# A hybrid diffusion layer on one core: the first stage starts on a quarter of its modulation, and two tiles walk the weight rows together

## The chip, the cores and the metric

The kernel runs on one core of a Trainium2 chip. The metric is device time in microseconds (us) of one execution. The engines are named as in the profile: PE is TensorE (matmuls; PEld is its weight load), DVE is VectorE, ACT is ScalarE, POOL is GpSimd, SP is SyncE, which here only issues DMAs. `L427` is line 427 of the kernel.

## What is computed

One layer of a diffusion backbone, for 256 context ("prompt") tokens and 2048 latent ("sample") tokens, all float32, model width 1024. Cut to the part that the change touches:

- Each stream has its modulation: `mod = silu(c) @ w_mod + b_mod`, with `c` the conditioning vector of the latent stream and `c_ctx` that of the prompt stream. It has six chunks of 1024 columns: shift1, scale1, gate1, shift2, scale2, gate2. The first stage needs only shift1 and scale1, which are columns 0 to 2047 of `w_mod` (1024 rows): 8.4 MB.
- `h = RMSNorm(x) * (1 + scale1) + shift1`, then one projection `h @ w_in`, whose 2048 columns are four groups of 512: queries, keys, values and the Fourier channels. `w_in` is another 8.4 MB.
- Queries and keys get an RMS norm per head; latent ones also get a rotary embedding. The Fourier channels go through a two-dimensional DFT, queries, keys and values through differential attention with four heads (512 cached and 2048 own keys for the latent stream: 2560, or five blocks of 512). In differential attention two softmaxes P0 and P1 are combined as P0 + factor x P1 before they meet the values.
- Then an output projection and a squared-ReLU MLP, both far behind the change.

## The kernel before

**Tiles and precision.** The tokens are 18 tiles of 128 rows: tiles 0 and 1 are the prompt, 2 to 17 the latent stream. A product in full precision is three matmuls (`mm3`, L85 to L88): each operand is split in a high part (a cast to a shorter format) and a low part (the rest), and high x high, high x low and low x high are added up in one PSUM bank. So a projection of one tile and one group, `proj(i, g)` (L237), is 8 row blocks k x 3 = 24 matmuls of 512 columns. Matmuls of plain float32 operands take two records each in the trace.

**Who sets the order.** Within a block `with tc.manual_schedule()` each engine gets its instructions as the code states them. Outside it a planner orders them by its own estimates. The first stage consists of a block by hand (L409 to L519), a loop that the planner orders (L521 to L550), and another block by hand for the last tile and the passage to the second stage (from L553).

**The block by hand (L409 to L519).**

- `setup_small` (L90) loads the conditioning vectors, biases and norm gains as rows and turns them into columns, `cols`, by one transpose.
- SP loads x0, then `w_mod` by rows: `wm0` to `wm7` (L416), each 128 rows x 2048 columns, 1 MB, with x1 between. They lie in pools of their own; W's tiles take their memory when they are done.
- The modulation of all 2048 columns: groups 0 to 2 of 512 columns each are PE matmuls with `cols` as the two-column stationary operand, and give a row for each stream (L427: 24 float32 matmuls); group 3 is summed on DVE, multiplying each `w_mod` row block by a column of `cols` (L431, L433: eight operations per stream) with a sum over partitions by PE with `ones` (L461). `mod_cols` (L452 to L456) copies the three rows out of PSUM and transposes them back into columns. L464 adds the bias to all, `mk_scale` (L170) makes `scale1`.
- `load_gains` (L109) loads the small vectors for the query and key norms by POOL's queue. `setup_gains` (L117) turns them into the tiles `qg`, `kg` and the factor `nlam`; in the middle of it ACT takes an exponential (L127) that DVE waits for. It stands behind `proj(1, 1)`.
- Tile 0 is transposed by PE and modulated on ACT and DVE (`h_mod`, L469), split into `HH[0]`. Tile 1's transposes follow (L487), its modulation is spread over the walk.
- `w_in` arrives in halves of a row block (`w_half`, L443: 128 x 1024, 512 KB) in a ring of six buffers. For each row block k, ACT casts four high parts (L495), DVE forms four low parts (L496), and PE multiplies tile 0 with all four groups (12 matmuls). The split weights, 64 tiles of 128 x 512, stay in SBUF through the first stage: group 2 in a pool on the left (`p1w`, L210), the other groups in a pool on the right (`p1wr`, L436), where they lie by group, then high or low, then k.
- Behind the walk, `f_post(0)`, `v_out(0)`, `proj(1, 0)`, the norms of tile 0's queries and keys, `proj(1, 1)`, and x3's load (L510 to L519).

**The loop** (L521) runs i from 1 to 16. For each tile: norm of the next tile, its projections in four groups, `transposed(i + 1)` (L228: eight transposes, modulation, split), the post-processing of each group, and the transposes of the queries and keys of tile i − 1 (`qk_T`). PSUM banks with the tag `pt` (two) carry all transposes. On odd tiles it also computes another 512 columns of the modulation, `mod_load` and `mod_group_v` (L155): DVE's weighted sums, then their sum over partitions on PE, all within the same tile.

**The passage to the second stage.** `right.close()` (L564) gives back the memory of the right weight tiles; `fa` takes it for the Fourier operands: `d_load` (L593) loads differences and reversed rows by SP, `dft` (L577) the DFT matrices by POOL's queue. A load can go when the last matmul that reads the memory it overwrites is done. `e2048` (L618) forms the DFT's operands from them.

**Attention's first group.** A group is 256 queries of a head. PE computes scores (L918), DVE takes maxima by block (L923), ACT the exponentials (L942), and `combine` forms P0 + factor x P1. As a rule POOL does that (L964 multiplies, L965 adds, in pieces of 1024 and 1536 columns). For the second half of the very first group `vcomb = 5` (L891): DVE combines all five blocks of 512 (L954).

Of the kernel before, what the change touches and what calls it, by code (L numbers as in the profile page):

```python
# [18 lines left out]
P = 128  # L19
# [21 lines left out]
def body(tc, a, out):  # L41
    nc = tc.nc
    ctx = ExitStack()
    with ctx:
# [98 lines left out]
        def mod_group(t2, pps, gi, w):  # L143

            pr = pps.tile([P, 512], F32, tag="pg", name=f"pr{gi}")
            for k in range(KD):
                nc.tensor.matmul(pr[0:2, :], cols[:, k:k + 9:8], w[k // 2][:, k % 2, :], start=(k == 0), stop=(k == KD - 1))
            r = t2(f"mr{gi}")
            nc.scalar.copy(r[0:2, :], pr[0:2, :])
            pm = pps.tile([P, 4, 2], F32, tag="pm", name=f"pm{gi}")  # L150
            for j in range(4):
                nc.tensor.transpose(pm[:, j, :], r[0:2, j * P:(j + 1) * P], ident[0:2, 0:2])
            mod_bias(gi, pm)

        def mod_group_v(t2, pps, gi, w):  # L155

            pm = pps.tile([P, 4, 2], F32, tag="pm", name=f"pm{gi}")
            for s in range(2):
                acc = t2(f"macc{gi}_{s}")
                for k in range(KD):  # L160
                    wk, sc = w[k // 2][:, k % 2, :], cols[:, 8 * s + k:8 * s + k + 1]
                    if k == 0:
                        nc.vector.tensor_scalar_mul(acc, wk, sc)
                    else:
                        nc.vector.scalar_tensor_tensor(acc, wk, sc, acc, op0=ALU.mult, op1=ALU.add)
                for j in range(4):
                    nc.tensor.matmul(pm[:, j, s:s + 1], acc[:, j * P:(j + 1) * P], ones, start=True, stop=True)
            mod_bias(gi, pm)
# [39 lines left out]
        with ExitStack() as c1:  # L208
            p1 = c1.enter_context(tc.tile_pool(name="p1", bufs=2))
            wp = c1.enter_context(tc.tile_pool(name="p1w", bufs=1))  # L210
# [197 lines left out]
            wsrc = a["w_in"][0].rearrange("(k p) n -> p k n", p=P)  # L408
            with tc.manual_schedule():  # L409
                with tc.tile_pool(name="p0r", bufs=3) as rows, tc.tile_pool(name="p0m", bufs=KD - 3, side="right") as more:  # L410
                    setup_small(p1, pps)
                    load(0)
                    wm = []
                    for k in range(KD):
                        wm.append((rows if k < 3 else more).tile([P, 2048], F32, tag="row", name=f"wm{k}"))
                        nc.sync.dma_start(wm[k], wmod[:, k, 0:2048])  # L416
                        if k == 2:
                            load(1)
                    norm(p1, X[0], "a0")
                    pr = [pp.tile([P, 512], F32, tag="pj", name=f"pr{gi}", bufs=4) for gi in range(4)]  # L420
                    pt0 = [pp.tile([P, 4, P], F32, tag="pt", name=f"pta0_{b}") for b in range(2)]
                    for k in range(KD):
                        nc.tensor.transpose(pt0[k // 4][:, k % 4, :], X[0][:, k * P:(k + 1) * P], ident)
                    acc = [t2(f"macc3_{s}") for s in range(2)]
                    for k in range(KD):
                        for gi in range(3):
                            nc.tensor.matmul(pr[gi][0:2, :], cols[:, k:k + 9:8], wm[k][:, gi * 512:gi * 512 + 512], start=(k == 0), stop=(k == KD - 1))  # L427
                        for s in range(2):
                            wk, sc = wm[k][:, 1536:2048], cols[:, 8 * s + k:8 * s + k + 1]
                            if k == 0:  # L430
                                nc.vector.tensor_scalar_mul(acc[s], wk, sc)  # L431
                            else:
                                nc.vector.scalar_tensor_tensor(acc[s], wk, sc, acc[s], op0=ALU.mult, op1=ALU.add)  # L433
                        if k == 4:
                            norm(p1, X[1], "a1")
                wr = right.enter_context(tc.tile_pool(name="p1wr", bufs=1, side="right", reuse_waits="tile"))  # L436
                W = {(g, x): [(wp if g == 2 else wr).tile([P, 512], F32R, tag=f"w{x}{g}_{k}", name=f"w{x}{g}_{k}") for k in range(KD)]
                     for g in (1, 0, 3, 2) for x in "hl"}
                wh, wl = ([W[g, x] for g in range(4)] for x in "hl")
                with tc.tile_pool(name="p0h", bufs=6, reuse_waits="tile") as halves:  # L440
                    wraw = []

                    def w_half(n):  # L443
# [4 lines left out]
                    for n in range(6):  # L448
                        w_half(n)
                    pm = pps.tile([P, 16, 2], F32, tag="pg", name="pm16")  # L450

                    def mod_cols(gi):  # L452
                        r = t2(f"mr{gi}")
                        (nc.vector.tensor_copy if gi == 1 else nc.scalar.copy)(r[0:2, :], pr[gi][0:2, :])
                        for j in range(4):
                            nc.tensor.transpose(pm[:, gi * 4 + j, :], r[0:2, j * P:(j + 1) * P], ident[0:2, 0:2])  # L456

                    mod_cols(0)
                    for s in range(2):
                        for j in range(4):  # L460
                            nc.tensor.matmul(pm[:, 12 + j, s:s + 1], acc[s][:, j * P:(j + 1) * P], ones, start=True, stop=True)  # L461
                    mod_cols(2)
                    mod_cols(1)
                    nc.vector.tensor_add(modc[:, 0:16, :], pm, cols[:, 32:48].unsqueeze(2).to_broadcast([P, 16, 2]))  # L464
                    mk_scale(scale1, 8, 80)
                    lq = load_gains(p1)
                    HH.update({i: tuple(p1.tile([P, KD, P], F32R, tag=f"h{x}", name=f"h{x}{i}") for x in "hl") for i in range(2)})

                    def h_mod(dst, pt, k, eng):  # L469
                        sc, sh = scale1[:, k, 1:2], modc[:, k, 1:2]  # L470
                        if eng is nc.vector:
                            nc.vector.tensor_scalar(dst, pt[:, k % 4, :], sc, sh, op0=ALU.mult, op1=ALU.add)
                        else:
                            nc.scalar.activation(dst, pt[:, k % 4, :], AF.Identity, bias=sh, scale=sc)

                    h0 = [t2(f"hTa0_{b}").rearrange("p (k t) -> p k t", k=4) for b in range(2)]
                    for k in range(4):
                        h_mod(h0[0][:, k, :], pt0[0], k, nc.scalar)
                        h_mod(h0[1][:, k, :], pt0[1], 4 + k, nc.vector)
                    for b in range(2):  # L480
                        hi, lo = (x[:, b * 4:b * 4 + 4, :] for x in HH[0])
                        nc.vector.tensor_copy(hi, h0[b])
                        nc.vector.tensor_sub(lo, h0[b], f32(hi))
                    X.pop(0)
                    pt1 = [pp.tile([P, 4, P], F32, tag="pt", name=f"pta1_{b}") for b in range(2)]
                    for k in range(KD):
                        nc.tensor.transpose(pt1[k // 4][:, k % 4, :], X[1][:, k * P:(k + 1) * P], ident)  # L487
                    X.pop(1)
                    PJ.update({(0, g): pp.tile([P, 512], F32, tag="pj", name=f"pj0_{g}", bufs=4) for g in (3, 2, 0, 1)})
                    hT = p1.tile([P, KD, P], F32, tag="hT", name="hTa1", bufs=1)  # L490
                    load(2)
                    for k in range(KD):
                        for g in range(4):
# [3 lines left out]
                            if g % 2 and 2 * k + g // 2 + 6 < 16:  # L497
                                w_half(2 * k + g // 2 + 6)
                        if 1 <= k < 5:
                            for x in (2 * k - 2, 2 * k - 1):  # L500
                                h_mod(hT[:, x, :], pt1[x // 4], x, nc.scalar)
                        if k == 5:
                            nc.scalar.copy(HH[1][0], hT)
                            nc.vector.tensor_sub(HH[1][1], hT, f32(HH[1][0]))
                        if k == 6:
                            norm(p1, X[2], "a2")
                        for g in range(4):
                            mm3(PJ[0, g], HH[0][0][:, k, :], HH[0][1][:, k, :], wh[g][k], wl[g][k], k == 0, k == KD - 1)
# [3 lines left out]
                proj(1, 0)  # L512
# [1393 lines left out]
```

## Time and profile before

| What | Value |
|---|---|
| median of 3 runs | 2973.66 us (2971.3 to 2975.22) |
| profiled execution | 2976.96 us, its span 2975.1 us |
| PE busy | 2910.2 us, 98% |
| DVE, ACT, POOL busy | 68%, 53%, 34% |
| mean granted clock of PE | 0.993 of full speed |

The span is what the trace covers. A row of the timeline reads: start in us, busy time in us, engine, line, operation, result<-operands, shape, number of instructions in the row, and in brackets the idle time of that engine ahead of it with what ended it. A row of the table by windows reads: the window, its length, then busy time and number of instructions for PE, PEld, DVE, ACT and POOL, then the granted clock, the share of the DMA engines' time and GB/s.

### The profile page before, as it was taken

How to read it: one execution, taken by the hardware profiler on the slowest of the kernel's cores; microseconds unless marked ns; L12 is line 12 of the kernel's file. 1: busy time of each engine (PE TensorE's matmuls, PEld its weight loads, DVE VectorE, ACT ScalarE, POOL GpSimd, SP SyncE). 2: the span in 40 equal slices, each digit the busy share in tenths (PEclk: the TensorE clock that was granted, in tenths of full speed). 3: DMA queues.
4: the chain of work that ended last, by engine and by line, in shares of the span. 5: the costliest groups of instructions: out<-in, count | busy, mean ns of one | idle time of the engine just before them, and what ended most of it. 6: DMA issues, size and time to landing. Idle time of an engine off the chain costs nothing.

```text
span 2975.1 us, 43755 instructions
## 1 busy us (share of the span) xinstructions
PE 2910.2 (98%) x15417; PEld 2518.0 (85%) x15417; DVE 2016.3 (68%) x3379; ACT 1568.3 (53%) x3540; POOL 1023.9 (34%) x839
## 2 busy tenths in 40 slices
PE   8999999989999999999999999999999999999999
PEld 4888887768888888888889999999999888888887
DVE  6666775678888888875458778777776344344554
ACT  4333322678888888864346556556555322232221
POOL 1111112169898989952222333333332000000000
PEclk9999999989999999999999999999999999999999
DMA  7777878512131211215686677676666454445563
GB/s 274 202 195 198 232 197 250 195 52 84 35 110 37 91 53 34 95 50 157 202 252 213 217 240 225 220 237 214 222 199 229 145 170 163 138 145 173 195 216 107
DMA packets 394414, 495.58 MB, mean 167 GB/s; under 512 B 26403, under 2 KB 307056, under 8 KB 391122
## 3 DMA queue, kind: packets, MB, share of 16 engines
q1 hardware_dynamic: 386560, 477.63, 50.5%
q0 software_dynamic: 2992, 7.28, 0.8%
q10 hardware_dynamic: 4642, 7.88, 0.8%
q8 instruction: 122, 2.00, 0.3%
q14 instruction: 98, 0.80, 0.1%
HBM read 315.20 MB, written 179.57 MB: 166 GB/s over the span
## 4 chain that ended last, share of the span: by engine, by line
PE 84%; ACT 8%; DVE 4%; DMA 2%; issue 1%; POOL 0%; SPq 0%; ACTq 0%; DVEq 0%; POOLq 0%
PE Ss L918 8%; PE ps L86 8%; PE ps L87 8%; PE ps L88 8%; PE pj L86 4%; PE pj L88 4%; PE pj L87 4%; PE pts L974 4%; ACT P1s L942 3%; PE po L88 2%; PE po L86 2%; PE po L87 2%; PE pA L1532 2%; PE pA L1534 2%; PE pA L1533 2%; PE pC L1534 2%
## 5 line engine op out<-in xcount | busy, mean ns | idle before, releaser
L923 DVE TENSOR_REDUCE mxs<-Ss 128x1 f32<-128x512 f32 x640 | 419.4, 687 | 86.8 <-PE Ss L918 77.9
L1227 DVE TENSOR_TENSOR sl<-sr,sh 128x768 fp32r<-128x768 f32 x168 | 161.8, 964 | 339.8 <-ACT sh L1226 339.3
L965 POOL TENSOR_TENSOR P0s<-P0s,P1s 128x1024 f32<-128x1024 f32 x124 | 365.7, 2949 | 10.4
L1226 ACT CAST sh<-sr 128x768 fp32r<-128x768 f32 x168 | 140.2, 835 | 424.9 <-PE ps L87 424.9
L942 ACT ACTIVATE P1s<-Ss,mxs 128x512 f32<-128x512 f32 x320 | 217.2, 694 | 69.3 <-DVE mxs L926 69.3
L1574 POOL TENSOR_TENSOR gs<-g,g 128x384 f32<-128x384 f32 x48 | 70.3, 1464 | 483.7 <-ACT g L1544 376.7
L86 PE MATMUL pj<-wh,hh 128*128 128x512 f32 x576 | 229.8, 399 | 0.7 <-ACT fo L374 0.7
L87 PE MATMUL ps<-tlT,sh 128*128 128x512 f32 x585 | 229.3, 392 | 0.0
L86 PE MATMUL ps<-thT,sh 128*128 128x512 f32 x585 | 229.2, 392 | 0.0
L87 PE MATMUL pj<-wl,hh 128*128 128x512 f32 x576 | 227.7, 395 | 0.7 <-DVE wl L496 0.7
L88 PE MATMUL ps<-thT,sl 128*128 128x512 f32 x585 | 227.7, 389 | 0.0
L88 PE MATMUL pj<-wh,hl 128*128 128x512 f32 x576 | 226.7, 394 | 0.0
L942 ACT ACTIVATE P0s<-Ss,mxs 128x512 f32<-128x512 f32 x320 | 215.8, 696 | 7.8 <-DVE mxs L926 7.7
L918 PE MATMUL Ss<-KS1s,Qs 128*128 128x512 f32 x640 | 199.9, 426 | 13.6 <-ACT P0s L942 11.1
L918 PE MATMUL Ss<-KS0s,Qs 128*128 128x512 f32 x640 | 198.7, 423 | 10.5 <-ACT P1s L942 9.4
L974 PEld LDWEIGHTS pts<-ident,P0s 128*128 128x128 f32 x1280 | 158.0, 141 | 51.7 <-ACT ahs L980 5.7
L974 PE MATMUL pts<-ident,P0s 128*128 128x128 f32 x1280 | 193.0, 274 | 6.3 <-DVE alp L1071 4.1
L1543 ACT ACTIVATE g<-uz 128x384 f32<-128x384 f32 x144 | 75.9, 527 | 207.1 <-DVE uz L1566 180.6
L964 POOL TENSOR_SCALAR P1s<-P1s,tots 128x1024 f32<-128x1024 f32 x124 | 166.7, 1344 | 5.6
L985 DVE TENSOR_TENSOR als<-pts,ahs 128x512 fp32r<-128x512 f32 x256 | 163.9, 681 | 5.3 <-ACT ahs L980 5.3
L86 PE MATMUL ps<-ophT,sh 128*128 128x512 f32 x423 | 165.9, 392 | 1.1 <-DVE uz L1566 1.1
L88 PE MATMUL ps<-ophT,sl 128*128 128x512 f32 x423 | 165.7, 392 | 0.0
(613 smaller groups left out, 8216.1 us busy)
## 6 DMA issues: line engine op xcount, KB each, us to landing
sr<-sd SPq DMA_DIRECT2D x84, 768.0 KB, 4.4
a<-in_w SPq DMA_DIRECT2D x184, 256.0 KB, 3.8
sd<-gs SPq DMA_DIRECT2D x192, 192.0 KB, 1.9
sd<-g SPq DMA_DIRECT2D x144, 192.0 KB, 4.1
wm<-in_w_mod SPq DMA_DIRECT2D x32, 512.0 KB, 5.3
Qs<-qd SPq DMA_DIRECT2D x32, 512.0 KB, 3.7
b<-in_w SPq DMA_DIRECT2D x64, 256.0 KB, 5.2
b<-tsum SPq DMA_DIRECT2D x64, 256.0 KB, 4.6
```

Source lines behind the costliest of these rows:

```text
L86: nc.tensor.matmul(ps, lh, rh, start=first, stop=False)
L87: nc.tensor.matmul(ps, lh, rl, start=False, stop=False)
L88: nc.tensor.matmul(ps, ll, rh, start=False, stop=last)
L918: nc.tensor.matmul(S[:, :w], self.Q[:, x, m, j * P:j * P + P], self.hd.KS[m][:, b * 512:b * 512 + w], start=(x == 0), stop=(x == 1))
L923: nc.vector.tensor_reduce(self.mx[j][:, m, b:b + 1], self.S[j, m, b], axis=AX.X, op=ALU.max)
L942: nc.scalar.activation(dst, S, AF.Exp, bias=self.mx[j][:, m, 6:7], accum_out=self.sm[j][:, m, b:b + 1])
L964: nc.gpsimd.tensor_scalar(p, p, tot[:, 3:4], 0.0, op0=ALU.mult, op1=ALU.add)
L965: nc.gpsimd.tensor_add(d, d, p)
L974: nc.tensor.transpose(pt[:, c:c + P], self.p0[j][:, (kb + t) * P:(kb + t + 1) * P], ident)
L985: nc.vector.tensor_sub(t, self.pt[kb], f32(self.A[kb][0]))
L1226: nc.scalar.copy(hi, src)
L1227: nc.vector.tensor_sub(lo, src, f32(hi))
```

## The change

- **The modulation in four parts.** Part s has 256 columns of shift1 and the same 256 of scale1, that is all that row blocks 2s and 2s + 1 of `h` need. Its eight loads of 128 x 512 (256 KB, each row in two pieces of 1 KB) go into buffers that are later tiles of W's row blocks 6, 5, 7 and, once part 0 is used up, 6 again (`WROW`).
- Parts 0 and 3 are PE rows (8 float32 matmuls each). Parts 1 and 2 are sums on DVE, one stream at a time (`mod_acc(part, stream)`: eight operations), each followed by a sum over partitions on PE (`mod_sum`: four float32 matmuls). Stream 1 is the prompt, so that the sums for stream 0 can come later. `mod_done` adds the bias and forms `scale1` for the part.
- **Two tiles walk together.** x0 and x1 are loaded first and both transposed into four PSUM banks; `h_part(s)` modulates and splits both for two row blocks. For each row block k, PE multiplies four groups for tile 0 and three for tile 1 (21 matmuls); tile 1's group 3 follows later as `proj(1, 3)`.
- The sums, rows and casts stand between the rows of the walk in an order written by hand; `setup_gains` moves ahead of row block 6's casts. Tile 2 is modulated within rows 6 and 7 (`x2_T`). The block by hand goes on through all four projections of tile 2.
- The loop begins at i = 2 with what is left of tile 2. The sums over partitions of `mod_group_v` become `mod_group_s` and move into the next tile.
- W's tiles are created by k, then group, then high or low, so they lie by row block in the right pool; the left pool `p1w` gets `reuse_waits="tile"`.
- `vcomb` of the first attention group goes from 5 to 2: DVE combines blocks 0 and 1, POOL multiplies and adds the last 1536 columns.

The diff, cut to its core:

```diff
-                    for k in range(KD):
-                        wm.append((rows if k < 3 else more).tile([P, 2048], F32, tag="row", name=f"wm{k}"))
-                        nc.sync.dma_start(wm[k], wmod[:, k, 0:2048])
...
-                W = {(g, x): [(wp if g == 2 else wr).tile([P, 512], F32R, tag=f"w{x}{g}_{k}", name=f"w{x}{g}_{k}") for k in range(KD)]
-                     for g in (1, 0, 3, 2) for x in "hl"}
...
+                WM, WROW = {}, (6, 5, 7, 6)
+                for k in range(KD):
+                    for g in (1, 0, 3, 2):
+                        for x in "hl":
+                            if k < 5:
+                                (wh if x == "h" else wl)[g][k] = w_tile(g, x, k, f"w{x}{g}_{k}")
+                            else:
+                                n = WROW.index(k)
+                                WM.setdefault(n, []).append(w_tile(g, x, k, f"wm{n}_{g}{x}"))
+                def wm_load(s):
...
+                    for k in range(KD):
+                        src = wmod[:, k, 0:2 * D].rearrange("p (t c) -> p t c", t=2)
+                        nc.sync.dma_start(f32(WM[s][k]).rearrange("p (t c) -> p t c", t=2), src[:, :, s * 256:s * 256 + 256])
...
+                def mod_mm(s, ks, pool, tag):
...
+                        nc.tensor.matmul(PR[s][0:2, :], cols[:, k:k + 9:8], f32(WM[s][k]), start=(k == 0), stop=(k == KD - 1))
...
+                def mod_acc(s, st):
+                    acc = ACC[s, st] = t2(f"macc{s}_{st}")
...
+                def mod_sum(s, st):
...
+                        nc.tensor.matmul(PM[s][:, j, st:st + 1], acc[:, j * P:(j + 1) * P], ones, start=True, stop=True)
...
+                    def h_part(s):
+                        for j in range(2):
+                            k = 2 * s + j
+                            nc.scalar.activation(xT[s][:, j], xT[s][:, j], AF.Identity, bias=modc[:, k, 1:2], scale=scale1[:, k, 1:2])
+                        for i in range(2):
+                            hi, lo = (x[:, 2 * s:2 * s + 2, :] for x in HH[i])
+                            nc.scalar.copy(hi, xT[s][:, :, i, :])
+                            nc.vector.tensor_sub(lo, xT[s][:, :, i, :], f32(hi))
...
+                    load(0)
+                    load(1)
+                    wm_load(0)
+                    wm_load(1)
+                    for _ in range(4):
+                        w_half()
+                    wm_load(2)
...
+                    mod_mm(0, range(0, 3), pp, "pt")
+                    x_T(0)
+                    x_T(1)
+                    mod_mm(0, range(3, KD), pp, "pt")
+                    wm_load(3)
+                    mod_acc(1, 1)
...
+                    w_cast(0)
+                    mod_row(0)
+                    mod_col(0)
+                    mod_done(0)
+                    h_part(0)
+                    mod_sum(1, 1)
...
+                    w_cast(2)
+                    mod_acc(1, 0)
+                    w_cast(3)
+                    load(2)
+                    load(3)
+                    mod_mm(3, range(KD), pps, "pm")
+                    mod_row(3)
+                    mod_acc(2, 1)
+                    pj_step(2, lambda: mod_col(3))
...
+                    mod_acc(2, 0)
+                    norm(p1, X[2], "a2")
+                    setup_gains(p1, lq)
+                    pj_step(4)
+                    pj_step(5)
+                    mod_sum(2, 0)
+                    mod_done(2, slice(0, 1))
+                    w_cast(6)
+                    w_cast(7)
...
+                q_T(0)
+                transposed(3)
+                v_split(1, 1, vo1, "v1")
+                proj(2, 2)
...
-            for i in range(1, LAST):
+            for i in range(2, LAST):
...
+                    if sums:
+                        mod_group_s(pps, *sums)
...
-                    self.vcomb = 5 if self.last else 5 if hd.h == hd.s == g == 0 else 0
+                    self.vcomb = 5 if self.last else 2 if hd.h == hd.s == g == 0 else 0
```

More of the change, by code (lines that the diff above doesn't have):

```diff
@@ L141, in mod_bias, with mod_group_v @@
             nc.vector.tensor_add(modc[:, gi * 4:gi * 4 + 4, :], pm, b)
[L143 to L157 removed]
+        def mod_group_v(t2, gi, w):
+            accs = []
             for s in range(2):
@@ L458, in body @@
[L458 to L466, printed above, removed]
```

232 lines of the change are left out of this document (145 added, 87 removed).

## The prediction

> **What bounds the kernel.** I read the page's head first, then the busy time by stage, then the timeline of the first 90 us and the places behind it that the diff touches. In the table the columns are window, length, busy time of PE, PEld, DVE, ACT and POOL with counts, granted clock, DMA share, GB/s.
>
> ```profile
> span 2975.1 us, 43755 instructions
> PE 2910.2 (98%) x15417; PEld 2518.0 (85%) x15417; DVE 2016.3 (68%) x3379; ACT 1568.3 (53%) x3540; POOL 1023.9 (34%) x839
> ```
>
> ```profile
> 0.00:40.00 40.00, 29.41 (x94) 10.16 (x94) 18.36 (x39) 8.03 (x16) 5.36 (x14) 0.98 0.89 337
> 40.00:67.00 27.00, 25.62 (x107) 20.29 (x105) 23.01 (x38) 23.89 (x51) 0.56 (x1) 0.90 0.64 224
> 67.00:90.00 23.00, 23.00 (x105) 18.99 (x106) 16.49 (x36) 7.51 (x15) 7.31 (x4) 1.00 0.62 172
> 90.00:485.00 395.00, 395.00 (x1928) 329.05 (x1927) 268.95 (x497) 120.29 (x257) 62.49 (x34) 1.00 0.77 202
> 590.00:620.00 30.00, 19.82 (x64) 12.86 (x63) 20.94 (x38) 16.75 (x48) 13.05 (x8) 0.72 0.05 18
> 620.00:2975.00 2355.00, 2320.91 (x12587) 2048.37 (x12585) 1601.08 (x2609) 1334.44 (x3024) 915.11 (x745) 1.00 0.47 155
> ```
>
> TensorE (PE) is the bound: 395.00 of 395 us in the rest of the first stage. So a microsecond saved ahead of 90 us arrives at 485 only if PE has no more work to do there, and PE work removed counts in full. Ahead of 90, PE is idle 10.6 + 1.4 + 0 = 12 us; this, and the modulation's matmuls, are all that the change to the first stage can win. In 590:620 PE is idle 10 us at clock 0.72: the second place that the diff touches.
>
> **The first stage, when it starts.** Before, the first projection waits for all of the modulation:
>
> ```profile
> 8.73 0.88 DVE L431 TENSOR_SCALAR macc<-wm,cols 128x512 f32<-128x512 f32 x2
> 10.76 22.77 PE L427 MATMUL pr<-wm,cols 128*2 128x512 f32 x48
> 31.86 0.57 ACT L454 COPY mr<-pr 2x512 f32<-2x512 f32 x1 [15.79 <-PE pr L427]
> 33.47 0.41 PE L456 MATMUL pm<-ident,mr 2*128 2x2 f32 x4
> 33.81 1.95 PE L461 MATMUL pm<-ones,macc 128*128 128x1 f32 x16
> 36.37 0.19 DVE L464 TENSOR_TENSOR modc<-pm,cols 128x32 f32<-128x32 f32 x1 [2.98 <-PE pm L456]
> 37.01 1.50 ACT L474 ACTIVATE hTa<-pta,modc,scale 128x128 f32<-128x128 f32 x4 [2.87 <-DVE scale L172]
> 38.40 4.26 ACT L495 CAST wh<-win 128x512 fp32r<-128x512 f32 x8
> 39.95 0.78 PE L86 MATMUL pj<-wh,hh 128*128 128x512 f32 x1
> 40.69 9.72 DVE L496 TENSOR_TENSOR wl<-win,wh 128x512 fp32r<-128x512 f32 x16
> 49.39 0.39 PE L86 MATMUL pj<-wh,hh 128*128 128x512 f32 x1
> 49.62 0.39 PE L87 MATMUL pj<-wl,hh 128*128 128x512 f32 x1
> 88.71 4.06 DVE L165 SCALAR_TENSOR_TENSOR macc<-wm,cols,macc 128x512 f32<-128x512 f32 x6
> ```
>
> After, it waits for x0, x1, modulation part 0 and W's row 0. SP's queue brings, in order, x0 and x1 (0.52 MB each), parts 0 and 1 (2.1 MB each) and two halves of row 0 (0.52 MB each). The old order had x0 and a 1.05 MB row there by 8.73 (L431 reads it): 1.57 MB. The other 3.67 MB ahead of W come in pieces of 1 KB. No load of this kind is in the trace, so I bound it:
>
> ```profile
> DMA packets 468, 3.36 MB, mean 420 GB/s; under 512 B 58, under 2 KB 58, under 8 KB 58
> DMA packets 543, 1.14 MB, mean 379 GB/s; under 512 B 41, under 2 KB 41, under 8 KB 542
> DMA packets 2559, 1.24 MB, mean 177 GB/s; under 512 B 144, under 2 KB 2559, under 8 KB 2559
> ```
>
> These are 16:24 (pieces of 4 KB and more), 97:100 (2 KB loads), 83:90 (512-byte stores). 1 KB loads lie between the last two; I take 350, near the 2 KB loads, because those too are loads of w_mod. That is 10.5 us, so 19.2; the halves at 420 take 1.25 each: 20.5 and 21.7. Two L495 casts of the last half (4.26/8 = 0.53): 22.8. ACT's row copy 0.57 (as L454): 23.4. Four transposes 0.41: 23.8. Three small DVE operations (36.37 to 37.01): 24.4. On ACT two 256-wide scalings and a 256-wide cast, about 0.5 each (1.50/4 = 0.38 for 128 columns, 0.53 for 512): 26. **The start moves from 40.0 to 26: −14.**
>
> **What PE then still owes.** Before, the whole modulation lay ahead of 40. After, behind 26: part 3 as 8 row matmuls, 16 of the 48 records, 16 × 0.43 (their spacing once warm) = 6.9; three sums of one stream each, 8 records where L461 has 16 for two (1.95): 1.0 each, 3.0; four transposes 0.4 (L456). **+10.3.** Tile 1's transposes and tile 2's are needed either way: 0. That PE starts cold is so in both: 0.
>
> **New stalls.** Rows that bear on them:
>
> ```profile
> 66.93 0.50 PE L86 MATMUL pj<-wh,hh 128*128 128x512 f32 x1 [0.69 <-ACT fo L374]
> 69.58 0.19 DVE L120 TENSOR_SCALAR qg<-qg 128x64 f32<-128x64 f32 x1
> 71.39 0.16 DVE L128 TENSOR_TENSOR nlam<-ls 128x1 f32<-128x1 f32 x1 [0.47 <-ACT ls L127]
> ```
>
> A sum of one stream on DVE is 0.44 + 7 × 0.68 (4.06/6) = 5.2. Between row 1 and row 6 DVE has three of them (15.6), five rows of lo parts (20 × 9.72/16 = 12.2), the splits and additions of parts 1 to 3 (about 12 small operations, 4), tile 2's norm (0.75) and the gains, moved here (69.58 to 71.6, 2.0): 34.5. PE has rows 2 to 5, each 7 groups × 3 matmuls × 0.23 (49.39 to 49.62) = 4.8, so 19.3; with part 3 and the sums 29.6. DVE falls behind by 4.9 in that stretch, less the lead with which it enters. The stall lies between 0 and one sum, 5.2; I take the middle, +2.7. Queued with it: the gains' exponential waits on ACT for DVE, and ACT's casts of row 6 stand behind it, so they too start late; that is inside the same 2.7. Then tile 0's query transposes and tile 3's eight follow each other on two slots that ACT must empty: bounds 0 and all eight evictions at L474's rate (four in 1.50), 3.0; the middle, with the hand-over: +1.7. The old wait at 66.93 goes: 0.69 by its row, 1.38 by the idle time of 40:67; −1.
>
> W's later rows hide: with parts 2 and 3 some 17.8 MB by row 7, at 350 about 54 us, and PE is there at 26 + 7 × 4.8 + 10 = 70. SP's other loads (x2, x3, x4) are needed after 60: 0. In the loop the sums' matmuls move one tile on: same count, 0. **First stage: −14 + 10.3 + 2.7 + 1.7 − 1 = −0.3.** A stall at row 6 lets ACT and DVE work off what the later one waits for (both have slack in 67:90), so not both come at the middle: I take **−1**, between −4.7 (none) and +3.5 (both at their upper ends).
>
> **The loads of the second stage.** Weight tiles on the right are now laid out row by row, so the buffers that replace them come free in another order.
>
> ```profile
> 474.40 0.32 SPq L593 DMA_DIRECT2D ds<-fdif  x1
> 483.32 1.11 SPq L593 DMA_DIRECT2D rv<-frev  x2
> 484.56 0.69 DVE L622 TENSOR_TENSOR e<-ds,rv 128x512 f32<-128x512 f32 x1
> 491.44 0.68 DVE L622 TENSOR_TENSOR e<-ds,rv 128x512 f32<-128x512 f32 x1
> ```
>
> The first load (474.40) goes when tile 17's projection 0 has read its last weight. Its memory now holds rows that projection 1 still reads, at k = 5 to 7: 18 matmuls × 0.23 = 4.1 later, and SP's queue behind it (rv, the reversed rows, the key and query stores) moves too. Cover: the first subtraction is at 484.56, 10 us after that issue; the last (491.44) is 7 after 483.32 + 1.11. Price 0 (cover holds) to +4.1 (none); nearest the cover: +1.
>
> **The first attention group.** Of five combining operations on DVE two stay; POOL takes 1536 columns.
>
> ```profile
> 588.27 1.55 POOL L964 TENSOR_SCALAR P1s<-P1s,tots 128x1536 f32<-128x1536 f32 x1
> 589.90 3.48 POOL L965 TENSOR_TENSOR P0s<-P0s,P1s 128x1536 f32<-128x1536 f32 x1
> 591.77 4.82 DVE L954 SCALAR_TENSOR_TENSOR P0s<-P1s,tots,P0s 128x512 f32<-128x512 f32 x5
> L954 DVE SCALAR_TENSOR_TENSOR P0s<-P1s,tots,P0s x10: 739/747/2167, 591.8 to 1307.5; 128x512 f32<-128x512 f32 x10
> 596.52 3.07 DVE L923 TENSOR_REDUCE mxs<-Ss 128x1 f32<-128x512 f32 x5
> 600.73 1.22 PE L918 MATMUL Ss<-KS0s,Qs 128*128 128x512 f32 x2 [5.29 <-ACT P1s L942]
> 606.11 0.34 POOL L948 TENSOR_SCALAR tots<-tots,nlam 128x1 f32<-128x1 f32 x1 [12.04 <-DVE tots L947]
> ```
>
> L954's five block the maxima (596.52), those ACT, and that PE (idle 5.29). The first takes 2.17 (the group's longest, 2167 ns), the other four 2.65, so three save 3 × 0.66 = **−2.0**. POOL's two operations, 1.55 + 3.48 = 5.0, fit into its 12.04 idle from 594.1 and end at 599.1, five ahead of its next work (606.11 − 2) and of the transposes behind that: 0. Were that cover gone, 5.0. The Trainium skill (SBUF — State Buffer, on the port that DVE and GpSimd share) says the one locks out the other; the trace agrees: the 2167 ns, against 747 else, belong to the one that meets POOL's addition (589.90 + 3.48 = 593.38).
>
> **Sum:** −1 + 1 − 2 = −2 against the profiled 2976.96 (span 2975.1). That execution is 3.3 above the median 2973.66, so **2971.7** for the median. A measurement here tells some 0.2%, 6 us, from no change: 2967.7 to 2979.6.
>
> **Rivals.**
> *Faster: the clock holds.* With 5.29 idle the clock falls to half:
>
> ```profile
> 600.00:610.00 10.00, 6.70 (x16) 4.41 (x17) 4.58 (x10) 7.29 (x21) 3.63 (x4) 0.50 0.00 0
> DVE mxs L923 <- PE Ss L918: 9.2, 12, 1.9
> ```
>
> If 3.3 idle keeps it at full, about half of DVE's 9.2 us of waiting for scores goes: −4.6, so 2967. Against it: 590:620 has gaps on every engine, so the clock may fall anyway. The Trainium skill (TensorE: Matmul & The Clock Gate, What's actually happening) has about 3.4 us without work as the window after which the clock halves, free-running; by it 3.3 is a coin's toss.
> *Slower: the 1 KB loads.* At 190 GB/s parts 0 and 1 (4.19 MB) take 22 instead of 12: the start is 36, +10, 2982. It decides from 8 us late, 4.19/20 = 210 GB/s. For it: the 177 row; against: that row is stores with half the piece. The Trainium skill (DMA: Bandwidth & Descriptors, Measured) asks for transfers of 1 MiB and more, and its table makes 256 KB, by my estimate, 2 us alone; 16 in a row would be 32 us and 2992. The 420 row, five 512 KB loads in flight, shows no such gap.
> *Covers gone:* row 6's stall 5.2 instead of 2.7 and the loads 4.1 instead of 1: +5.6, 2977.3, no measurable change by itself.
> *Nothing at all:* the table's 395.00 of 395 speaks for it, since a moved wait is worth nothing there; 2973.7, inside my sum's own range.
>
> **Chances.** My sum 0.38 (own range 2968 to 2976). The clock holds, 0.25; 0.17 of it past 6 us. First stage without the two stalls, −4.4, 2967.3: 0.13, past 6 us. Slow loads 0.12. Covers gone 0.12: with POOL's 5.0 too, as the order by hand has more places than I priced, 2982; 0.08 of it past 6 us. Faster 0.17 + 0.13 = 0.30, slower 0.12 + 0.08 = 0.20, same 0.50. Range 2962 (clock held and no stalls: 2971.7 − 4.6 − 4.4 = 2962.7) to 2982.
>
> **What would show it.** First L86-line matmul at 26 (35: slow loads; 22: fast ones); PE idle near row 6, at 65 to 72, of 0 to 5; end of projections at 484 to 485; first load of the second stage at 478; L954 two, PE's gap before 600 of 3.3; granted clock of 600:610 0.5 or 1. The prediction is wrong if PE's busy time grows, or if the order written by hand stalls at a place that I haven't named.

## The result, and the profile after

| | before | after |
|---|---|---|
| median of 6 runs each | 2974.73 us (2971.3 to 2977.13) | 2993.74 us (2991.0 to 2995.16) |
| span of the profiled execution | 2975.1 us | 2992.0 us |
| PE busy | 2910.2 us | 2908.6 us |

The ratio is 1.0063 (95% interval 1.0052 to 1.0074): the change makes the kernel 19 us slower. The forecast was 2971.7 with a range of 2962 to 2982, so the time lies outside it and on the other side. PE does 1.6 us less work; what came in is waiting.

First the table by windows of the changed kernel, with the columns and boundaries of the one in the prediction (it holds fewer windows, as the second stage no longer begins at 485).

```profile
0.00:40.00 40.00, 20.68 (x66) 11.22 (x67) 18.82 (x42) 14.65 (x28) 5.34 (x14) 0.83 0.94 294
40.00:67.00 27.00, 27.00 (x114) 17.56 (x113) 24.41 (x46) 12.54 (x25) 0.00 (x0) 1.00 0.76 279
67.00:90.00 23.00, 19.77 (x87) 15.99 (x86) 14.11 (x31) 9.55 (x22) 0.56 (x1) 0.93 0.25 85
90.00:485.00 395.00, 391.35 (x1898) 325.26 (x1897) 278.30 (x511) 123.76 (x266) 64.60 (x32) 0.99 0.77 200
```

PE's idle time ahead of 90 grew from 12.0 to 22.6 us, and the stretch that was full before, 395.00 of 395, has 3.65 of idle time and a clock of 0.99. The timeline of the changed kernel shows the places: each row is the instruction behind a gap of PE (in brackets), except the casts, DVE's operations and the load.

```profile
10.20 1.87 PE L435 MATMUL pr<-wm_1h,cols 128*2 128x512 f32 x2 [3.25 <-DMA wm_1h<-in_w_mod]
27.14 2.41 ACT L519 CAST wh<-win 128x512 fp32r<-128x512 f32 x4 [10.14 <-DMA win<-in_w_in]
30.08 0.58 PE L445 MATMUL pm<-ident,mr 2*128 2x2 f32 x4 [9.16 <-ACT mr L439]
32.94 0.79 PE L86 MATMUL pj<-wh,hh 128*128 128x512 f32 x1 [0.15 <-ACT hh L509]
77.07 0.50 PE L86 MATMUL pj<-wh,hh 128*128 128x512 f32 x1 [2.53 <-ACT wh L519]
78.27 0.59 PE L87 MATMUL pj<-wl,hh 128*128 128x512 f32 x1 [0.70 <-DVE wl L520]
109.96 0.66 PE L193 MATMUL pta<-ident,x 128*128 128x128 f32 x4 [1.60 <-ACT hTa L196]
418.02 1.05 PE L161 MATMUL pm<-ones,macc 128*128 128x1 f32 x8 [1.85 <-DVE macc L153]
493.12 0.32 SPq L716 DMA_DIRECT2D ds<-fdif  x1
505.17 0.75 PE L86 MATMUL pabE<-c,E_h 128*128 128x512 f32 x1 [5.21 <-DMA c<-in_c]
609.76 2.83 DVE L1077 SCALAR_TENSOR_TENSOR P0s<-P1s,tots,P0s 128x512 f32<-128x512 f32 x2
616.72 0.72 PE L1041 MATMUL Ss<-KS0s,Qs 128*128 128x512 f32 x2 [3.29 <-ACT P1s L1065]
```

How the difference builds up is best read at fixed amounts of work. The first stage has 1728 projection matmuls in either kernel; the table gives the start of the one that is reached, from the two timelines.

| reached | before | after | after less before |
|---|---|---|---|
| the first projection matmul | 39.95 | 32.94 | −7.0 |
| the 127th (after's first of row 6) | 73.92 | 77.07 | +3.2 |
| the 301st | 118.22 | 125.99 | +7.8 |
| the 1401st | 402.26 | 410.97 | +8.7 |
| the 1451st | 415.63 | 429.99 | +14.4 |
| end of the last | 485.59 | 499.96 | +14.4 |
| the first attention score | 571.29 | 589.69 | +18.4 |
| end of the span | 2975.1 | 2992.0 | +16.9 |

So the loss sits in four places: by row 6, behind row 6, in one tile of the loop, and in the passage to the second stage; from the first score to the end 1.6 comes back. (The last row has 16.9 and the medians 19, because the profiled execution of the kernel before, 2976.96, lies 2.2 above its median.)

### The profile page after: what moved, and what is told of

Same layout as the page of the kernel before. It is cut to its first block, busy times and chain, and to the rows that moved or that the text cites. A ratio compares the mean times of both kernels' runs of the same rounds, so it can differ in the third digit from the quotient of the medians.

```text
span 2992.0 us, 43836 instructions
## 1 busy us (share of the span) xinstructions
PE 2908.6 (97%) x15413; PEld 2518.6 (84%) x15413; DVE 2028.5 (68%) x3407; ACT 1569.7 (52%) x3545; POOL 1028.6 (34%) x841
## 4 chain that ended last, share of the span: by engine, by line
PE 79%; ACT 8%; DVE 6%; DMA 4%; issue 1%; POOL 0%; SPq 0%; ACTq 0%; DVEq 0%; POOLq 0%
PE Ss L1041 8%; PE ps L86 8%; PE ps L87 8%; PE ps L88 8%; PE pts L1097 4%; PE pj L86 3%; PE pj L88 3%; PE pj L87 3%; ACT P1s L1065 3%; PE po L88 2%; PE po L86 2%; PE po L87 2%; PE pB L1655 2%; PE pA L1655 2%; PE pC L1657 2%; DVE mxs L1046 2%
## 5 line engine op out<-in xcount | busy, mean ns | idle before, releaser
L1088 POOL TENSOR_TENSOR P0s<-P0s,P1s 128x1536 f32<-128x1536 f32 (+1 forms) x125 | 370.2, 2961 | 10.4
L1087 POOL TENSOR_SCALAR P1s<-P1s,tots 128x1536 f32<-128x1536 f32 (+1 forms) x125 | 168.3, 1347 | 5.7
```

What stands on the lines that cost most here:

```text
L1087: nc.gpsimd.tensor_scalar(p, p, tot[:, 3:4], 0.0, op0=ALU.mult, op1=ALU.add)
L1088: nc.gpsimd.tensor_add(d, d, p)
```

## The experiments

Unless it is said otherwise, each kernel is the changed one with the edit shown, looked at in one profile. Stretches that an edit doesn't touch repeat to about 1 us: the end of the projections lies between 499.2 and 501.5 in the changed kernel and the seven whose edit leaves both tile 16's load and the trip at row 6 (below) in place.

**The broadcasts of the gains.** What held the start? In the changed kernel between 10 and 20 us, from the view of its DMA queues:

```profile
DMA packets 2220, 2.15 MB, mean 215 GB/s; under 512 B 214, under 2 KB 2125, under 8 KB 2220
q1 hardware_dynamic: 2034, 1.96, 60.2%
q0 software_dynamic: 186, 0.19, 37.6%
```

POOL's queue moves 0.19 MB, a tenth of SP's 1.96, and takes 37.6% of the DMA engines' time. These are the small vectors of `load_gains`, each spread to 128 partitions; before, POOL issued them from 21.97 on, when W was loading well ahead of its use. Here it issues them from 9.60: on POOL's queue they stand behind a step of tile 1's norm (L83) in both kernels, and as x1 is now loaded first, that step starts at 9.10 instead of 21.46.

```diff
-                    lq = load_gains(p1)
                     mod_mm(0, range(0, 3), pp, "pt")
...
                     wm_load(3)
+                    lq = load_gains(p1)      # with nc.sync in place of nc.gpsimd
```

> The changed kernel, but the six broadcast loads of the small gain vectors leave POOL's queue and go to SP's, behind part 3 of the modulation. In the changed kernel they are issued from 9.60 on and fall into the loads that the start waits for; in its first 30 us POOL's queue takes 12.6% of 16 DMA engines, 3.8 us of all of them, for 0.20 MB. Theory 1 (these broadcasts hold up the start): the first projection moves from 32.94 to about 29.2. Theory 2 (pieces of 1 KB are slow by themselves): it stays at 32.9 within 0.5.

The same view of this kernel, and its rows for row 3 of W:

```profile
DMA packets 3309, 3.56 MB, mean 356 GB/s; under 512 B 202, under 2 KB 3187, under 8 KB 3309
q1 hardware_dynamic: 3309, 3.56, 109.1%
```

```profile
46.00 2.42 ACT L519 CAST wh<-win 128x512 fp32r<-128x512 f32 x4 [11.23 <-DMA win<-in_w_in]
55.27 1.87 PE L461 MATMUL pm<-ones,macc 128*128 128x1 f32 x8 [3.64 <-DVE modc L467]
```

The rate between 10 and 20 goes from 215 to 356 GB/s and the first projection to 26.99, against 32.94 in the changed kernel and 31.2 to 32.9 in the others that leave the start alone: 4 to 6 us, theory 1 holds with more than its price. But the end of the projections is 500.93. Row 3's casts start at 46.0, where the changed kernel has them at 47.10: the broadcasts, now on SP's queue, still lie ahead of that load. In this kernel's table by windows, while they go:

```profile
39.00:42.00 3.00, 3.00 (x8) 0.59 (x7) 2.37 (x4) 0.00 (x0) 0.00 (x0) 1.00 0.17 36
```

PE waits 3.64 at 55.27, and row 6 starts at 77.33, in the changed kernel at 77.07. The start alone is worth nothing. The edit moves the broadcasts to another queue and to a later time at once; which of the two frees the start was not told apart.

**The size of the pieces.**

```diff
-                        src = wmod[:, k, 0:2 * D].rearrange("p (t c) -> p t c", t=2)
-                        nc.sync.dma_start(f32(WM[s][k]).rearrange(...), src[:, :, s * 256:s * 256 + 256])
+                        nc.sync.dma_start(f32(WM[s][k]), wmod[:, k, s * 512:s * 512 + 512])
```

> The changed kernel, but each modulation part is loaded as 512 neighbouring columns, in pieces of 2 KB instead of two of 1 KB: the same bytes and the same number of loads from the wrong columns, so the outputs are not the reference's. Theory 2 (the 1 KB pieces are slow): the first projection moves from 32.94 to 27 to 29. Theory 1 (the broadcasts): it stays at 32 to 33. If both count, some 30 to 31.

The first projection is at 30.93, against 31.2 to 32.9 in the kernels that leave these loads and the broadcasts alone: at most 2 us, the end 499.28. That lies in the range that was set for both theories counting, so the pieces have a small share. The broadcasts have the larger one: with 2 KB pieces and the broadcasts in place the rate between 10 and 20 is 242 GB/s, with 1 KB pieces and the broadcasts gone 356.

**The sums in their old place.**

```diff
-                    sums = mod_group_v(t2, mg, wm)
+                    mod_group_s(pps, *mod_group_v(t2, mg, wm))
```

(and the call in the next tile goes.)

> The changed kernel, but in the loop the sums over partitions stand in the same tile as the weighted sums, as before. Theory 1 (the sum that moved one tile on waits for DVE): PE's gap of 1.85 at 418 and the slow clock behind it (3.3 by the matmuls' spacing) go, and the last projection ends some 5 us earlier than 499.96, at about 495. Theory 2 (DVE is as late in either place, and PE waits elsewhere): the end moves by less than 1.

PE still waits, 1.53 at 397.8 and 1.22 for the sum at 418.9; the end is 500.85. Theory 1 falls: DVE is late in either place.

**One late load.** Why is DVE late there? The planner's order on SP's queue has moved tile 16's x behind the reversed rows, six transfers later than before. The first line is the load in the kernel before; in the changed kernel its square on ACT waits for it:

```profile
364.98 0.34 SPq L225 DMA_DIRECT2D x<-in_x_sample  x1
382.26 1.27 SPq L219 DMA_DIRECT2D x<-in_x_sample  x1
388.03 1.06 ACT L180 ACTIVATE nsqa<-x 128x1024 bf16<-128x1024 f32 x1 [7.09 <-DMA x<-in_x_sample]
```

```diff
-                nc.sync.dma_start(X[i], ...)
+                (nc.gpsimd if i == 16 else nc.sync).dma_start(X[i], ...)
```

> The changed kernel, but one load, tile 16's x, goes by POOL's queue instead of SP's, where the planner has put it behind six more transfers than before (issued at 382.26, its norm waits for it to 388). No other engine's order changes. Theory 1 (this late load starts the chain norm, DVE, sum over partitions that PE waits for at 418): PE's gap of 1.85 at 418 and the slow clock behind it (3.3) go, the last projection ends at about 495 instead of 499.96. Theory 2 (DVE is late because of its own queue): the gap stays within 0.7 and the end within 1.

In this kernel:

```profile
362.76 1.06 ACT L180 ACTIVATE nsqa<-x 128x1024 bf16<-128x1024 f32 x1 [2.16 <-DMA x<-in_x_sample]
```

and in its table by windows:

```profile
370.00:420.00 50.00, 50.00 (x252) 41.92 (x252) 35.48 (x68) 15.58 (x34) 8.36 (x5) 1.00 0.84 224
```

The square comes 25 us earlier and PE is full. The gap is gone, the end is 494.27, 5.7 earlier, and nothing else in the order was touched. Theory 1 holds.

**Row 6.** Two kernels take work out of DVE's queue ahead of row 6.

```diff
-                    for k in range(KD):
+                    for k in range(1 if (s, st) == (2, 0) else KD):     # sum20_short
```

> The changed kernel, but the weighted sum of part 2 for stream 0 takes only the first of its eight operations, so the latent stream's modulation lacks seven eighths of that part. It takes 5.5 us out of DVE's queue ahead of row 6. Theory 1 (DVE's queue from row 3 to row 6 sets when row 6 starts): PE's gaps at 77 (2.53 and 0.70) and the slow clock behind them (1.9) go, the last projection ends at 494.5 to 496. Theory 2 (W's row 6 or ACT's casts are late anyway): the gap stays above 2.

```diff
                     norm(p1, X[2], "a2")
-                    setup_gains(p1, lq)                                 # setup_late
...
                 proj(2, 0)
+                setup_gains(p1, lq)
```

> The changed kernel, but the gains are set up behind tile 2's first projection, where they stood relative to the query norm before, and not ahead of row 6's casts. Theory 1 (DVE's queue sets row 6, and the gains' 2.1 us are part of it): the gaps at 77 shrink from 3.23 to about 1.1, and the last projection ends 2 to 4 earlier than 499.96. Theory 2 (the exponential on ACT, in front of the casts, matters and DVE's work does not): the gaps vanish altogether. Theory 3: what is moved comes back as a wait behind tile 2's projection, and the end moves by less than 1.

Theory 1 of each falls: one gap of 2.73 is left in both, and the ends are 499.22 and 499.87. These are the numbers of sum20_short's theory 2 and setup_late's theory 3, but the traces show another reason. First the changed kernel itself:

```profile
73.59 0.95 PE L461 MATMUL pm<-ones,macc 128*128 128x1 f32 x8
74.75 0.20 ACT L127 ACTIVATE ls<-ls 128x2 f32<-128x2 f32 x1 [8.39 <-DVE ls L126]
74.86 4.24 ACT L519 CAST wh<-win 128x512 fp32r<-128x512 f32 x8
75.25 0.15 DVE L467 TENSOR_TENSOR modc<-pm,cols 128x4 f32<-128x4 f32 x1
```

DVE comes to part 2's addition (L467) at 75.25, straight from the last operation of the gains, and PE's sum, which that addition needs, has been done since 74.54. PE's gap at 77.07 ends with ACT's casts; these stand behind the exponential, and it waits for DVE. So here DVE's queue is the hold. The timeline of sum20_short, DVE and PE ahead of row 6, shows what comes up when that queue is lighter:

```profile
72.41 0.95 PE L461 MATMUL pm<-ones,macc 128*128 128x1 f32 x8
73.40 0.16 DVE L467 TENSOR_TENSOR modc<-pm,cols 128x4 f32<-128x4 f32 x1 [4.40 <-PE pm L461]
73.88 4.91 DVE L520 TENSOR_TENSOR wl<-win,wh 128x512 fp32r<-128x512 f32 x8
76.43 0.50 PE L87 MATMUL pj<-wl,hh 128*128 128x512 f32 x1 [2.73 <-DVE wl L520]
```

DVE is idle for 4.40 us: it waits for the sum on PE that stands behind row 5, and only then forms row 6's low parts, which PE needs. With the hand-written order PE can't pass from row 5 to row 6 without a trip to DVE and back. (In setup_late the same wait is 1.28.) So two holds lie one behind the other, and taking away the first alone gains nothing. The next kernel takes away both: besides the gains, it turns the addition and the low parts around on DVE:

```diff
                     mod_sum(2, 0)
-                    mod_done(2, slice(0, 1))
                     w_cast(6)
+                    mod_done(2, slice(0, 1))
```

(with the gains set up late as above.)

> The changed kernel with the gains set up late, as in setup_late, and on DVE the low parts of row 6 ahead of the addition of part 2's latent sum (mod_done). In the changed kernel that addition waits for the sum on PE that stands behind row 5, and the low parts wait behind it, so PE cannot go from row 5 to row 6 without a trip to DVE. Theory 1 (this trip, then DVE's queue, makes the gaps at 77): with both taken away the gaps fall from 3.23 to under 0.7 and row 7 follows without a new one; the clock behind them stays up, and the last projection ends 4 to 5 earlier than 499.96. Theory 2 (W's row 6 itself is late): a gap of over 2 stays.

In this kernel:

```profile
74.03 0.50 PE L87 MATMUL pj<-wl,hh 128*128 128x512 f32 x1 [1.52 <-DVE wl L520]
```

Row 6 starts at 72.04 instead of 77.07, one gap of 1.52 is left, and the end is 491.73, 8.2 earlier where 4 to 5 were expected. Of that, 5.0 come by row 6 and 5.8 by the 301st matmul (120.19); the rest is the loop's wait, which shrank to 0.87, for a reason that was not looked for. The changed kernel and the four whose edits are felt only behind row 6 (sums_same, x16_pool, layout_old, vcomb_5) reach row 6 between 75.7 and 77.1, so at least 3.7 of the 5.0 are clear of that spread. The gap was expected under 0.7, so theory 1 holds in the main and not wholly: DVE's sum and norm still end at 71.5. What the expectation says of the changed kernel, that its addition waits for PE's sum, is not so by the lines above; that wait is in sum20_short and setup_late. The turn without the late gains was not run.

**The broadcasts once more.** On top of that kernel the gains are loaded last:

```diff
                     w_cast(5)
+                    lq = load_gains(p1)      # on SP's queue, behind the last load of W
```

> The kernel row_6_free, and the gains' broadcast loads go by SP's queue behind the last load of W. Theory 1 (the queue of loads up to W's row 3, then DVE's chain of sums and low parts, sets row 6 in the changed kernel, not the start): the start moves from 32 to about 27 as in gains_late, W's row 3 comes some 3 earlier than in row_6_free, and the last projection ends 2 to 4 earlier than in row_6_free. Theory 2 (the start has no hold on the end, as gains_late seemed to show): the end stays within 1 of row_6_free's.

Now the casts of row 3 start at 41.87, 3.5 earlier than the 45.40 of row6_free, and row 6 at 68.29, 3.75 earlier. Up to row 6 theory 1 holds: the loads up to W's row 3, then DVE, set it. The end is 493.92 all the same, 2.2 later than row6_free's where 2 to 4 earlier was expected: the loop takes it back, with gaps of 1.24 at 390.0 and 2.39 at 412.3. Both are gone in all_mended (below), where tile 16's load is moved too.

**The layout.**

```diff
-                for k in range(KD):
-                    for g in (1, 0, 3, 2):
-                        for x in "hl":
+                for g in (1, 0, 3, 2):
+                    for x in "hl":
+                        for k in range(KD):
```

> The changed kernel, but W's tiles lie in memory by group, high or low, then k, as before. Theory 1 (the layout delays the second stage's loads): from the end of the last projection to the first score, 89.73 in the changed kernel and 85.70 before, it is 85.7 within 0.7. Theory 2 (the loads are late for another reason, such as more traffic): it stays at 89 to 90.

The first load in this kernel, and a wait of DVE in the changed kernel that this one doesn't have:

```profile
488.07 0.32 SPq L716 DMA_DIRECT2D ds<-fdif  x1
512.25 0.69 DVE L745 TENSOR_TENSOR e<-ds,rv 128x512 f32<-128x512 f32 x1 [6.33 <-DMA rv<-frev]
```

The first load goes out 11.2 ahead of the last projection's end (before: 11.2; after: 6.8), and the stretch from that end to the first score is 85.43. Theory 1 holds: the layout by row costs 4.3 us.

**The combining operations.** One kernel undoes this part of the change, one does it alone.

```diff
-                    self.vcomb = 5 if self.last else 2 if hd.h == hd.s == g == 0 else 0
+                    self.vcomb = 5 if self.last else 5 if hd.h == hd.s == g == 0 else 0
```

> The changed kernel, but with all five blocks of the first attention group's second half combined on DVE, as before. By the sum of the prediction PE's gap of 3.29 ahead of the blocked scores goes back to 5.29, and from the first score to the end it takes 2.0 to 2.4 us longer than the changed kernel's 2397.90. If the difference were due to something else, it stays within 0.7.

> The kernel before with this one part of the change: two blocks of the first attention group's second half combined on DVE instead of five. By the prediction's sum 2.0 us, by the pair of the changed kernel and vcomb_5 1.4 to 2.4 us less from the first score to the end; median 2.0 us less, which is under what the comparison can tell (0.07%). If the gain were due to the other order of the first stage, nothing.

The gap in vcomb_5:

```profile
621.18 1.22 PE L1041 MATMUL Ss<-KS0s,Qs 128*128 128x512 f32 x2 [5.28 <-ACT P1s L1065]
```

It is 5.28 with five operations and 3.29 with two. From the first score to the end of the last matmul it takes 2399.27 against 2397.90. In the kernel before, with two, the gap is 3.31 and that stretch 2395.68 against 2399.46; the median of 11 runs is 2972.19 against 2973.38 of 21, ratio 0.9998 (0.9989 to 1.0007). But in the changed kernel and the ten others made from it that have two operations, the stretch varies from 2396.48 to 2399.76, so neither difference is clear of that. The gap shrinks by the 2.0 that was forecast; whether the kernel gains from it, the runs can't tell.

**All together.** Row 6 freed, the gains loaded last, W's tiles laid out by group, tile 16's x on POOL's queue:

> The changed kernel with row 6 freed, the gains loaded last, W's tiles laid out by group as before, and tile 16's x by POOL's queue. By the runs so far: last projection at 499.96 - 5.7 (tile 16's x) - 4.5 (row 6) - 2 to 4 (broadcasts) = 486 to 488, the second stage 85.5, the attention as in the changed kernel: span 2969 to 2973, against 2975 before: within 0.2% of the kernel before, 0 to 0.2% faster. If a new wait comes up behind those taken away, the last projection ends past 491 and the kernel is slower than before.

```profile
0.00:40.00 40.00, 26.23 (x89) 15.20 (x90) 24.57 (x50) 15.58 (x29) 1.80 (x8) 0.87 0.98 334
40.00:67.00 27.00, 26.99 (x114) 17.93 (x113) 22.93 (x44) 15.23 (x30) 0.00 (x0) 1.00 0.60 219
67.00:90.00 23.00, 21.31 (x102) 17.43 (x101) 15.60 (x36) 7.86 (x19) 6.34 (x3) 1.00 0.32 112
```

The last projection ends at 485.72, where it ended before (485.59), the second stage takes 86.64, and the median of 11 runs is 2973.43 against 2973.38: ratio 1.0002 (0.9993 to 1.0011). Expected were 486 to 488 and 85.5. These four causes carry the loss, as far as the timing can tell. The run also shows what the change is worth without them: it starts 12.8 earlier than the kernel before (27.20) and has nothing of it at 485. That is what the prediction's sum for the first stage said, −0.3: −12.8 at the start, 10.3 owed, gaps of 1.69 and 1.60, 1.38 of old gaps gone give −0.6, and measured is +0.1.

## Why the prediction was wrong, step by step

- **The bound** was read rightly: PE sets the time, and its gaps ahead of 485 arrive there in full.
- **The start, −14, to 26.** It came to 32.94. The bytes, the rate of 350 (356 measured once the queue was alone) and the chain of casts, row, columns and split were right: without the broadcasts the start is at 26.99. What failed is that the walk left out POOL's queue. The loads of `load_gains` stand there behind a step of tile 1's norm, which comes 12 us earlier because x1 is loaded first, and so they go out 12 us earlier and into the loads that the start waits for. The rival of slow loads had the direction, but the 1 KB pieces have at most 2 us of the 7.
- **What the start is worth.** "W's later rows hide" put row 7 at 54 and never looked at row 3. Its load stands in the queue behind 13.6 MB (x0 and x1, all four parts, rows 0 to 2, itself) and the broadcasts: 47 us. From there DVE's chain runs to row 6. So even a start at 27 gave no earlier end until that load came earlier as well.
- **What PE owes, +10.3**, stands: part 3's 16 records run at 0.43 (44.90 to 51.8), a sum's eight take 0.95, and with the start at 27 the kernel is no earlier at 485.
- **The stall at row 6, +2.7**: 3.23 by the two gaps. The reason held: DVE's queue, then the exponential, then the casts. That the size came so near is partly luck, as 2.7 was the middle of 0 to 5.2. Two things were missing. Behind this hold lies a second one, PE's sum behind row 5, so that less work on DVE gains nothing by itself. And a gap costs more than itself: the clock behind it was 0.50 for 3.4 us, which is 1.7 us of work.
- **The transposes behind each other, +1.7**: 1.60 in every kernel that has them, on ACT's eviction as forecast; here too the size was the middle of a range, 0 to 3.0.
- **The loop, 0.** This is the largest miss of a term that was put at nothing: 5.65 between the 1401st and the 1451st matmul, 13.37 us before and 19.02 after. "Same count, 0" looked at the matmuls and not at SP's order. The planner placed one load six transfers later; with the load elsewhere the stretch takes 13.36.
- **The second stage's loads, +1**, between 0 and 4.1: it is 4.0, the upper end (89.73 against 85.69), and the old layout gives it back. The cover for the first subtraction held, the one for the later ones did not. The last reversed rows go out at 502.07, behind the DFT matrices, which POOL issues from 497.69 on (with the old layout at 496.80, just ahead of 496.99), and DVE waits 6.33 us for them, where it waited for none before. PE's wait for the DFT matrices, 5.21 against 3.22 before, is no measure of the layout: it is 3.92 with the old one, and 3.30 in sums_same, which has the new one.
- **The combining operations, −2.0**: 2.0 at the gap. How much of it reaches the end is not shown.
- **The rival of a held clock** fell. The matmuls behind the gap of 3.29 ran at full clock (0.72 for two, where before they took 1.22), and then it dropped to 0.50 all the same.

In sum, of the 15.4 us between the forecast −1 for the first stage and the measured +14.4, the start has 7.0, the loop 5.65, the slow clock behind row 6 about 1.7, row 6's gap 0.5. These come from PE's own timeline, where they add up; the experiments show that the first can't be had back alone. What stays open: 0.9 us between the 301st and the 1401st matmul, which all_mended has as well, and why the planner chose that place for tile 16's load. The 1.60 of the transposes was not taken away by itself: moving them gives the planner another order for the whole loop.

## What to carry to other kernels

When an order by hand is moved, every engine's queue has to be walked again, also those that seem idle: a DMA that stood behind something late goes out as soon as that comes early, and it takes its share of the transfer that the critical path waits for. An earlier start is worth only as much as the slowest later arrival allows, so follow each operand of the next stages and not the first alone. An order in which engine A waits for B's answer between two of its own steps costs a round trip even when both have time to spare; look for it wherever a small result is folded in ahead of a large one. And a hold that is taken away may uncover the next at nearly the same place: that an experiment gains nothing does not clear what it took away.

## What the runs showed of the hardware

Loads that spread one small row over 128 partitions are dear for their bytes. On POOL's queue six of them, 0.2 MB, took 37.6% of the DMA engines' time over 10 us, and the rate of everything fell to 215 GB/s; with them gone it was 356 GB/s for the same 1 KB pieces. On SP's queue, in gains_late, they cost in another way: they take little of the DMA engines' time, but hardly anything else moves while they go, 36 GB/s at a share of 0.17 from 39 to 42.

The slow clock can follow a gap of PE that is short. In the changed kernel, around the gap of 1.85 us at 418:

```profile
416.00:418.00 2.00, 0.17 (x1) 0.00 (x0) 2.00 (x5) 0.00 (x0) 0.00 (x0) 1.00 1.02 198
418.00:420.00 2.00, 1.78 (x14) 1.69 (x14) 1.91 (x4) 0.86 (x2) 0.00 (x0) 0.97 0.60 120
420.00:422.00 2.00, 2.00 (x7) 1.71 (x8) 0.00 (x0) 0.34 (x1) 1.95 (x1) 0.50 0.99 193
424.00:426.00 2.00, 2.00 (x6) 1.56 (x5) 2.00 (x5) 0.00 (x0) 0.00 (x0) 0.50 0.88 123
```

The granted clock is 0.50 from 419.9 to 426.7, so the wait costs 1.85 and then 3.4 more. Between the gap and the next projection matmul, at 420.50, PE has only the sixteen records of one-column sums, which seem to count for little: with them it has had no other matmul since 416.17, for 4.3 us. In row6_free the gap ahead of the same sums is 0.87, it is 3.3 us without another matmul, and the clock falls as well:

```profile
411.00:413.00 2.00, 1.41 (x12) 1.33 (x12) 2.00 (x4) 0.53 (x1) 0.00 (x0) 1.00 0.78 173
413.00:415.00 2.00, 2.00 (x10) 1.81 (x10) 0.27 (x2) 0.68 (x2) 1.59 (x1) 0.57 0.91 181
415.00:417.00 2.00, 2.00 (x7) 1.57 (x6) 0.64 (x2) 0.00 (x0) 1.32 (x1) 0.58 0.71 137
```

Without a gap, in all_mended, the same sixteen take 1.84 us and the clock stays at 1.00; behind the gap of 1.60 at 109.96 in the changed kernel it stayed at 1.00 too. The Trainium skill (TensorE: Matmul & The Clock Gate, What's actually happening) gives a free-running window of about 3.4 us. The case agrees in so far as the stretches at 0.50 last 3.4 us (behind row 6) or twice that (behind 418), and as the clock fell behind 4.3 and 3.3 us without a matmul wider than one column; that such matmuls count as idle is a reading of these two places, and no run tests it by itself.
